# A fifth slot in the third weight ring, routing tiles in the loop's buffers, and a residual added at another place, in a hybrid mixer and mixture-of-experts layer

## The chip, the core and the metric

The kernel runs on one core of a Trainium2 chip. The metric is the device time of one execution in microseconds (us), the median of several runs; a profile of one execution says where that time goes. PE is TensorE, PEld its weight load, DVE is VectorE, ACT is ScalarE, POOL is GpSimd, and SP is the engine whose queue (SPq) issues nearly all loads here.

## What is computed

One decoder layer for 256 tokens of width 1024, in float32. The first sub-layer mixes tokens (a gated linear attention and a pooling branch) and ends with a LayerNorm; the second is a mixture of 64 small experts with a shared expert, and ends with another LayerNorm. Cut to what matters here:

```python
h = layer_norm(ALPHA * x + mixer(x), ln1_g, ln1_b)          # first sub-layer
scores = sigmoid(h @ w_router)                              # (256, 64)
biased = scores + router_bias
# the best 4 of 8 groups of experts, by the sum of a group's two best,
# then the best 8 experts in them; weights = scores of these, normed, * 2.5
routed = sum over experts e of
         gate[t, e] * (silu(h @ w_exp_gate[e]) * (h @ w_exp_up[e])) @ w_exp_down[e]
shared = (silu(h @ w_sh_gate) * (h @ w_sh_up)) @ w_sh_down
out = layer_norm(ALPHA * h + routed + shared, ln2_g, ln2_b)
```

Each expert has three matrices of 1024 x 256 or 256 x 1024, 1 MB each, so the experts alone are 192 MB that have to be read once.

## The kernel before

All weights come in pieces of 1 MB in one fixed list (`loads`), the order in which they are used: the columns of w_in, the matrices of the branches, w_sh_gate, and then for the experts two at a time `gate`, `gate`, `up`, `up`, and the `down` matrices four at a time. The class Ring hands each next load to the slot that has come free: `open` fills a pool of slots, `done` says that a load is used up and issues the next one of the list into its slot. The slots are those of ring1 (8, one of them held by x at first), ring2 (6, opened when the branches' tiles are gone), ring3 (NR3 = 4, L814, opened when the first sub-layer's last buffers are gone) and xt (2, tiles xTh and xTl), 20 in all; one more load, `lent`, borrows another buffer once. All these issues stand in SP's queue, in the order of the program, and each waits until what its slot held before has been read. ring3 is closed at q = 4 (L1202): its slots aren't filled again, and from q = 7 their memory holds `overflow()` (a branch for the case that an expert has more than 32 tokens of a tile, L1078, not taken with these inputs) and the tiles of the shared expert (`shp`).

Between the sub-layers stands the routing: router scores, the bias, group choice and the choice of 8 experts run on DVE as a chain of small steps (L855 to L881), their tiles lie in a pool of their own, `mid`, and PE meanwhile computes the shared expert's gate. Then the first `gather` (L895) picks the tokens of eight experts by matrix products.

The loop (L1183) has 16 rounds q of four experts. Each round has two `gate_up` (64 matmuls each, L1031), the transposes of their result (`hidden_t`), the `down` products of the round before in two halves of the columns (L1056), whose results ACT and DVE split into two parts (L1061, L1062), and `scatter` (L1073, L1074), which adds them to four PSUM banks `acc[t, half]`, one for each tile t of 128 tokens and each half of the columns. What is to be scattered waits in the list `ready`, and `flush` empties it. In rounds 2 to 5 `residual(t, c)` (L975) also puts ALPHA * h into `ready`, for 256 columns at a time; it needs ln1_g and ln1_b with the same row on all 128 partitions, and `load_rows(c)` (L990) fetches them so from HBM, two loads for each c, at q = 0 (c = 0 and 1), 3 and 4. The other rows, of ln2, are loaded to one partition (`lnr`, L1226, at q = 12) and spread by POOL (L1231).

The last round's downs are done in three pieces of columns, 512, 256 and 256. Both tiles are taken in turn, piece by piece (L1248). `scatter` takes a half's statistics as soon as it is whole (L1076); then come mean and deviation, and four halves are normalised on three engines (L1268) and stored from SP's queue.

Of the kernel before, what the change touches and what calls it, by code (L numbers as in the profile page):

```python
# [16 lines left out]
NQ = E // 4  # L17
# [5 lines left out]
NR1, NR2, NR3 = 8, 6, 4  # L23
# [3 lines left out]
ROWS, RES = {0: (0, 1), 3: (2,), 4: (3,)}, {2: 0, 3: 1, 4: 2, 5: 3}  # L27

C_ID, C_MASK, C_TRI, C_IOTA, C_RC, C_SLOT, C_OWN = 0, 128, 320, 448, 480, 544, 545
C_COLS = 549  # L30
# [80 lines left out]
def body(ctx, tc, A, out, dbg=lambda *a: None, stop=None):  # L111
# [96 lines left out]
    cst = keep.tile([128, C_COLS], FT, name="cst")  # L208
# [19 lines left out]
    onesb = keep.tile([128, 128], BF, name="onesb")  # L228
# [6 lines left out]
    gla = tc.alloc_tile_pool(name="gla", bufs=1)  # L235

# [15 lines left out]
    for n in range(2):  # L252
# [3 lines left out]
    nc.sync.dma_start(cst[:, C_MASK:], A["cst"][:, C_MASK:])  # L256
# [6 lines left out]
    nc.sync.dma_start(wr, A["w_router"][0].rearrange("(p k) e -> p k e", k=8))  # L263
    nc.sync.dma_start(rbias, bass.AP(tensor=A["router_bias"].tensor, offset=A["router_bias"].offset,
                                     ap=[[0, 128], [1, E]]))
    V.memset(one_c, 1.0)
    V.memset(eps_rms, RMS_EPS)
    V.memset(eps_ln, LN_EPS)
    V.memset(onesb, 1.0)
    G.tensor_copy(identb, ident)  # L270
    G.tensor_copy(trib, cst[:, C_TRI:C_TRI + 128])
# [78 lines left out]
    def gla_steps():  # L350
# [25 lines left out]
        def small_scores(lv, lhs, rhs):  # L376
            p = bank("b", (8, 32), "gs")
            for jt in range(2):
                for h in range(H):
                    for b in range(4):  # L380
                        t0 = 128 * jt + 32 * b
                        PE.matmul(p[32 * b:32 * b + 32, 4 * jt + h], lhs[:, h, t0:t0 + 32],
                                  rhs[:, h, t0:t0 + 32], start=True, stop=True,
                                  tile_position=(0, 32 * b))
            m = cst[:, None, C_MASK + 32 * lv:C_MASK + 32 * (lv + 1)].to_broadcast([128, 8, 32])
# [145 lines left out]
    def pool_steps():  # L531
        yield "late2"
        sw, pl, pm, mx = {-1: uT}, {}, {}, {}
        for i in range(8):
# [10 lines left out]
            if 0 <= i - 1 < 4:  # L545
# [3 lines left out]
                V.tensor_mul(pl[n][:, :16], t[:, n, :16], cst[:, C_RC + 16 * n:C_RC + 16 * (n + 1)])  # L549
# [269 lines left out]
    sc = mid.tile([128, 2, E], FT, name="sc")  # L819
# [23 lines left out]
    pr = mid.tile([128, 2, 8, 4, 8], FT, name="pr", tag="pr", bufs=1)  # L843
    gs = mid.tile([128, 2, 8], FT, name="gs")
    top = mid.tile([128, 2, 8], FT, name="top")
    gr = mid.tile([128, 2, 8], FT, name="gr")
    pen = mid.tile([128, 2, 8], FT, name="pen")
    mx8 = mid.tile([128, 2, 8], FT, name="mx8")
    mbr = moe.tile([128, 2, 16, 8], FT, name="mbr", tag="PT", bufs=2)
    mb, mr = mbr[:, 0], mbr[:, 1]  # L850
    sel = mid.tile([128, 2, E], FT, name="sel")
    selb = mid.tile([128, 2, E], BF, name="selb")
# [79 lines left out]
    PE.matmul(pc[:1], onesb[:, 0:1], selb, start=True, stop=True)  # L932
# [18 lines left out]
    ssum = mid.tile([128, 2], FT, name="ssum")  # L951
    gt = mid.tile([128, 2, E], FT, name="gt")
# [21 lines left out]

    def residual(t, c):  # L975
# [4 lines left out]
        tmp = moe.tile([128, FF], FT, name="tmp", tag="sg", bufs=1).rearrange("p (q k) -> p k q", k=8)  # L980
# [202 lines left out]
    for q in range(NQ):  # L1183
        last = q == NQ - 1
        for c in ROWS.get(q, ()):
            load_rows(c)
        if q in RES:
            ready.append(residual(0, RES[q]))
# [8 lines left out]
        if q in RES:  # L1197
            ready.append(residual(1, RES[q]))
        if q == 7:
            rest.release()  # L1200
        if q == CLOSE3 - 3:
            ring.closed.add("w3")  # L1202
        if q == CLOSE3:
# [16 lines left out]
        if q == SH_DOWN:  # L1220
            shared_down()
            shp.release()
# [34 lines left out]
    flush()  # L1257
    for t in range(2):
        m = mv[:, t]
        V.bn_aggr(m[:, 0:2], st2[:, t])  # L1260
        S.activation(m[:, 2:3], m[:, 1:2], AF.Sqrt, bias=eps_ln)
    for t in range(2):
        m = mv[:, t]
        V.reciprocal(m[:, 3:4], m[:, 2:3])
        if t:
            V.scalar_tensor_tensor(m[:, 4:5], m[:, 0:1], -1.0, m[:, 3:4], op0=OP.mult, op1=OP.mult)

    def finish(t, n, engines):  # L1268
        m, ot, hs_ = mv[:, t], o[t][:, halves[n]], halves[n]
        if engines is None:  # L1270
            V.scalar_tensor_tensor(ot, acc[t, n], m[:, 0:1], g2[:, hs_], op0=OP.subtract, op1=OP.mult)
            V.scalar_tensor_tensor(ot, ot, m[:, 3:4], b2[:, hs_], op0=OP.mult, op1=OP.add)
        else:
            S.activation(ot, acc[t, n], AF.Identity, scale=m[:, 3:4], bias=m[:, 4:5])
            engines[0].tensor_mul(ot, ot, g2[:, hs_])
            engines[1].tensor_add(ot, ot, b2[:, hs_])

    finish(1, 0, (G, G))
    finish(0, 0, None)
    finish(0, 1, None)  # L1280
    finish(1, 1, (V, V))
    for t in range(2):
        for hs_ in halves:
            nc.sync.dma_start(out[0, 128 * t:128 * (t + 1), hs_], o[t][:, hs_])
# [26 lines left out]
```

## Time and profile before

| | us |
|---|---|
| median of 3 runs (lowest, highest) | 701.03 (700.68, 701.27) |
| the profiled execution | 701.09 |
| its span, first to last instruction | 699.2 |
| PE busy in the span | 675.0 (97%) |
| DVE, ACT, POOL busy | 291.4, 228.0, 60.9 |
| DMA: bytes, mean rate | 243.07 MB, 348 GB/s |

A busy PE isn't a PE that decides: matmuls overlap, and their ends are modelled. The page of the profile has the span in 40 slices, a chain of work that is followed back from the last instruction to what released each step, and groups of instructions; other views give single instructions in order of time, or the busy time of each engine in chosen windows with the granted TensorE clock (PEclk, 1.00 is full), the mean busy share of the 16 DMA engines, and the rate.

### The profile page before, as it was taken

How to read it: one execution, taken by the hardware profiler on the slowest of the kernel's cores; microseconds unless marked ns; L12 is line 12 of the kernel's file. 1: busy time of each engine (PE TensorE's matmuls, PEld its weight loads, DVE VectorE, ACT ScalarE, POOL GpSimd, SP SyncE). 2: the span in 40 equal slices, each digit the busy share in tenths (PEclk: the TensorE clock that was granted, in tenths of full speed). 3: DMA queues.
4: the chain of work that ended last, by engine and by line, in shares of the span. 5: the costliest groups of instructions: out<-in, count | busy, mean ns of one | idle time of the engine just before them, and what ended most of it. 6: DMA issues, size and time to landing. Idle time of an engine off the chain costs nothing.

```text
span 699.2 us, 13708 instructions
## 1 busy us (share of the span) xinstructions
PE 675.0 (97%) x5948; PEld 478.3 (68%) x5948; DVE 291.4 (42%) x476; ACT 228.0 (33%) x352; POOL 60.9 (9%) x51
## 2 busy tenths in 40 slices
PE   8999999999999999999999999999999899899993
PEld 8999999999999756556556546555645555364541
DVE  3688745946676523354343123311212221121216
ACT  4554646764444213123223113210312221131232
POOL 1053404600002000000000002000000000000001
PEclk9999999999999999999999999999999999999998
DMA  9995543499677799999999999999999999999981
GB/s 284 295 350 155 175 127 122 128 382 420 238 267 299 274 425 412 422 419 406 420 418 421 418 419 419 419 423 418 419 421 419 420 419 419 422 419 416 403 294 60
DMA packets 67889, 243.07 MB, mean 348 GB/s; under 512 B 6994, under 2 KB 37458, under 8 KB 44020
## 3 DMA queue, kind: packets, MB, share of 16 engines
q1 hardware_dynamic: 67684, 242.11, 88.3%
q8 instruction: 47, 0.77, 0.5%
q10 hardware_dynamic: 144, 0.07, 0.1%
q14 instruction: 14, 0.11, 0.0%
HBM read 241.11 MB, written 1.05 MB: 346 GB/s over the span
## 4 chain that ended last, share of the span: by engine, by line
PE 59%; DMA 38%; DVE 2%; issue 0%; ACT 0%; SPq 0%; DVEq 0%
PE pgu L1031 15%; DMA w<-in_w_exp_up 15%; DMA w<-in_w_exp_down 12%; DMA w<-in_w_exp_gate 9%; PE py L1056 7%; PE proj L291 6%; PE proj L293 6%; PE proj L292 6%; DMA xTl<-in_w_exp_down 3%; PE pgat L905 2%; PE acc L1073 1%; PE yg L293 1%; PE yg L292 1%; PE yg L291 1%; PE mix L291 1%; PE mix L292 1%
## 5 line engine op out<-in xcount | busy, mean ns | idle before, releaser
L1031 PE MATMUL pgu<-w,xg 128*64 128x256 f32 x1824 | 228.8, 381 | 6.8 <-DMA w<-in_w_exp_up 6.0
L1031 PEld LDWEIGHTS pgu<-w,xg 128*64 128x64 f32 x1824 | 142.5, 137 | 94.2 <-ACT Y L1061 11.7
L1056 PE MATMUL py<-w,ht 128*32 128x512 f32 (+1 forms) x904 | 121.7, 591 | 2.3 <-DMA w<-in_w_exp_down 1.8
L288 DVE TENSOR_TENSOR sl<-w,sh 128x1024 fp32r<-128x1024 f32 (+1 forms) x63 | 80.3, 1282 | 41.9 <-ACT sh L287 41.7
L1038 DVE TENSOR_TENSOR h<-sg,pgu 128x256 f32<-128x256 f32 x32 | 13.5, 422 | 187.7 <-ACT sg L1037 128.5
L1062 DVE SCALAR_TENSOR_TENSOR Y<-py,gsl,Y 128x512 fp32r<-128x512 f32 (+1 forms) x66 | 48.1, 734 | 96.2 <-ACT Y L1061 96.1
L291 PE MATMUL proj<-xTh,sh 128*128 128x256 f32 x288 | 83.0, 288 | 0.3 <-ACT sh L287 0.3
L293 PE MATMUL proj<-xTh,sl 128*128 128x256 f32 x288 | 81.5, 283 | 0.2 <-DVE sl L288 0.2
L1061 ACT ACTIVATE Y<-py,gsl 128x512 fp32r<-128x512 f32 (+1 forms) x66 | 44.2, 673 | 114.4 <-PE py L1056 114.3
L292 PE MATMUL proj<-xTl,sh 128*128 128x256 f32 x288 | 81.0, 281 | 0.0
L1037 ACT ACTIVATE sg<-pgu 128x256 f32<-128x256 f32 x32 | 12.3, 384 | 198.1 <-PE pgu L1031 198.1
L287 ACT ACTIVATE sh<-w 128x1024 fp32r<-128x1024 f32 (+1 forms) x63 | 64.3, 1028 | 35.0 <-PE proj L293 13.4
L1056 PEld LDWEIGHTS py<-w,ht 128*32 128x32 f32 x904 | 31.6, 111 | 57.1 <-issue 48.8
L291 PEld LDWEIGHTS proj<-xTh,sh 128*128 128x128 f32 x288 | 54.1, 188 | 1.1 <-ACT sh L287 0.5
L292 PEld LDWEIGHTS proj<-xTl,sh 128*128 128x128 f32 x288 | 54.6, 190 | 0.3 <-DVE xTl L288 0.2
L293 PEld LDWEIGHTS proj<-xTh,sl 128*128 128x128 f32 x288 | 53.9, 187 | 0.4 <-DVE sl L288 0.4
L1056 PE MATMUL py<-xTl,ht 128*32 128x512 f32 (+1 forms) x104 | 44.1, 562 | 0.0
L1031 PE MATMUL pgu<-xTh,xg 128*64 128x256 f32 x144 | 32.7, 380 | 0.0
L777 DVE TENSOR_SCALAR xg<-pgat,cols_sb 128x512 f32<-128x512 f32 x32 | 25.7, 809 | 13.9 <-PE pgat L905 11.5
L905 PE MATMUL pgat<-P,xl 128*128 128x256 f32 x128 | 30.6, 283 | 0.3 <-DVE xl L941 0.3
L905 PE MATMUL pgat<-P,xh 128*128 128x256 f32 x128 | 30.3, 283 | 0.0
L779 ACT ACTIVATE xg<-pgat,cols_sb 128x512 f32<-128x512 f32 x32 | 24.7, 777 | 17.3 <-PE pgat L905 17.3
(269 smaller groups left out, 948.5 us busy)
## 6 DMA issues: line engine op xcount, KB each, us to landing
w<-in_w_exp_gate SPq DMA_DIRECT2D x59, 1024.0 KB, 15.8
w<-in_w_exp_up SPq DMA_DIRECT2D x55, 1024.0 KB, 19.0
w<-in_w_exp_down SPq DMA_DIRECT2D x49, 1024.0 KB, 19.8
w<-in_w_in SPq DMA_DIRECT2D x21, 1024.0 KB, 7.2
xTh<-in_w_exp_up SPq DMA_DIRECT2D x6, 1024.0 KB, 17.3
xTl<-in_w_exp_down SPq DMA_DIRECT2D x5, 1024.0 KB, 16.2
w<-in_w_exp_down SPq DMA_DIRECT2D x9, 512.0 KB, 15.4
w<-in_w_gla_up SPq DMA_DIRECT2D x4, 1024.0 KB, 10.9
```

The costliest lines, as they stand in the source:

```text
L287: S.activation(hi, src, AF.Copy)
L288: eng.tensor_sub(lo, src, hi.bitcast(FT))
L291: PE.matmul(o, ah, bh, start=start, stop=False, skip_group_check=shared_bank)
L292: PE.matmul(o, ah, bl, start=False, stop=False, skip_group_check=shared_bank)
L293: PE.matmul(o, al, bh, start=False, stop=stop, skip_group_check=shared_bank)
L777: V.tensor_scalar(dst, p, g1T[:, k:k + 1], b1T[:, k:k + 1], op0=OP.mult, op1=OP.add)
L779: S.activation(dst, p, AF.Identity, bias=b1T[:, k:k + 1], scale=g1T[:, k:k + 1])
L905: PE.matmul(p[k][:, t].rearrange("p e s -> p (e s)"), part[:, t, k], P8[o][:, t].rearrange("p e s -> p (e s)"), start=part is xh, stop=par ...
L1031: PE.matmul(p[64 * c:64 * c + 64, g], xg[:, k, e].rearrange("p t s -> p (t s)"), w[c][:, k], start=k == 0, stop=k == 7, tile_position=(0, ...
L1056: PE.matmul(p[32 * c:32 * c + 32], HT[2 * q + c // 2][:, j, c % 2, t], ring.get(li["down", 4 * q + c])[:, j, cs], start=j == 0, stop=j == ...
L1061: S.activation(hi, p, AF.Copy, scale=g)
L1062: V.scalar_tensor_tensor(lo, p, g, hi.bitcast(FT), op0=OP.mult, op1=OP.subtract)
```

## The change

- `NR3` is 5: ring3 has a fifth slot. Room for it comes from smaller constants (the part that only the first sub-layer needs, `cst1`, moves to the branches' pool `right`), from `rbias`, which lies in R1's first half until R1 is written, and from `mid`, which is gone: the routing's tiles lie in buffers that the loop uses later (`ht`, `PT`, the rest of the tile of x2T).
- The router's bias is loaded ahead of the router's weights; the constants come in two loads instead of one; a one-column tile of ones is set besides the 128x128 one.
- `load_rows` and its eight loads are gone. At q = 7, behind `overflow()`, two loads bring ln1_g and ln1_b to one partition, and POOL spreads them to all (`spread`).
- `residual` runs at q = 9 and 10, on 512 columns at a time, and takes h from the shared expert's tiles `SH[t]`, so that the addition of xh and xl falls away; `shp` is released at q = 11 instead of 10.
- At the end tile 0's three pieces come before tile 1's second and third, tile 0's mean and deviation are taken while tile 1's last piece is computed, and the four halves are spread over the engines in another way.

```diff
-NR1, NR2, NR3 = 8, 6, 4
+NR1, NR2, NR3 = 8, 6, 5
-ROWS, RES = {0: (0, 1), 3: (2,), 4: (3,)}, {2: 0, 3: 1, 4: 2, 5: 3}
+RES = 9
...
-    rbias = keep.tile([128, E], FT, name="rbias")
     R1 = keep.tile([128, 2, E], FT, name="R1")
+    rbias = R1[:, 0]
...
-    nc.sync.dma_start(cst[:, C_MASK:], A["cst"][:, C_MASK:])
+    nc.sync.dma_start(cst1, A["cst"][:, C_KEPT:])
+    nc.sync.dma_start(cst[:, C_IOTA:], A["cst"][:, C_IOTA:C_KEPT])
...
-    mid = tc.alloc_tile_pool(name="mid", bufs=1, reuse_waits="tile")
+    ht = [moe.tile([128, n], dt, name="mid", tag="ht", bufs=3) for n, dt in ((256, FT), (512, BF), (256, FT))]
+    mbr = moe.tile([128, 2, 16, 8], FT, name="mbr", tag="PT", bufs=2)
+    scgt = moe.tile([128, 2, 2, E], FT, name="scgt", tag="PT", bufs=2)
...
     def residual(t, c):
-        qs = slice(32 * c, 32 * (c + 1))
-        lo, hi = (rest.tile([128, 256], FR, name=n) for n in ("reslo", "reshi"))
+        qs = slice(64 * c, 64 * (c + 1))
+        tmp = shp.tile([128, 8, 64], FT, name="tmp")
+        hi, lo = (shp.tile([128, 512], FR, name=n) for n in ("reshi", "reslo"))
-        V.tensor_add(tmp, xh[:, t, :, qs].bitcast(FT), xl[:, t, :, qs].bitcast(FT))
-        for n, op in (("g", OP.mult), ("b", OP.add)):
-            V.tensor_tensor(tmp, tmp, rows1[n, c].rearrange("p (q k) -> p k q", k=8), op)
+        g, b = (rows1[n].rearrange("p (q k) -> p k q", k=8)[:, :, qs] for n in "gb")
+        V.tensor_mul(tmp, SH[t][:, :, qs], g)
+        V.tensor_add(tmp, tmp, b)
         S.activation(hv, tmp, AF.Copy, scale=ALPHA)
         V.scalar_tensor_tensor(lv, tmp, ALPHA, hv.bitcast(FT), op0=OP.mult, op1=OP.subtract)
-        return None, t, slice(256 * c, 256 * (c + 1)), hi, lo
+        return None, t, halves[c], hi, lo
...
-        for c in ROWS.get(q, ()):
-            load_rows(c)
-        if q in RES:
-            ready.append(residual(0, RES[q]))
+        if RES <= q < RES + 2:
+            ready.append(residual(0, q - RES))
+        if q == RES + 2:
+            shp.release()
...
+            one = shp.tile([1, 2, D], FT, name="rowone")
+            for i, n in enumerate("gb"):
+                nc.sync.dma_start(one[:, i], A["ln1_" + n])
+                rows1[n] = shp.tile([128, D], FT, name="row" + n)
+            spread([rows1[n] for n in "gb"], one)
...
-    for cs in pieces_of(NQ - 1):
-        for t in range(2):
-            flush(1)
-            ready.append(down(NQ - 1, t, cs))
-    done_downs(NQ - 1)
...
-    finish(1, 0, (G, G))
-    finish(0, 0, None)
-    finish(0, 1, None)
-    finish(1, 1, (V, V))
+    c0, c1, c2 = pieces_of(NQ - 1)
+    for t, cs in ((0, c0), (1, c0), (0, c1), (0, c2), (1, c1)):
+        flush(1)
+        ready.append(down(NQ - 1, t, cs))
+    flush(1)
+    moments(0)
+    scales(0)
+    ready.append(down(NQ - 1, 1, c2))
+    done_downs(NQ - 1)
+    normed(0, 1)
+    affine2(0, 1, G)
+    centre(0, 0)
+    flush()
+    moments(1)
+    shift(0, 0)
+    scales(1)
+    normed(1, 1)
+    centre(1, 0)
+    shift(1, 0)
+    affine2(1, 1, V)
```

Here `moments` is the mean and the square root, `scales` the reciprocal and one small product, `centre` and `shift` are DVE's two steps on a half, `normed` is one ACT step, and `affine2` a multiplication and an addition on the engine named.

## Rows read from the trace of the kernel before

**Rows 1.** The page, the span in 40 equal slices: PE's busy tenths, and GB/s.
```profile
PE   8999999999999999999999999999999899899993
...
GB/s 284 295 350 155 175 127 122 128 382 420 238 267 299 274 425 412 422 419 406 420 418 421 418 419 419 419 423 418 419 421 419 420 419 419 422 419 416 403 294 60
```

**Rows 2.** The chain that ended last: start in us, length in us, what.
```profile
381.74 7.06 PE pgu L1031 x64
...
401.02 19.68 DMA w<-in_w_exp_up
...
665.63 3.67 PE pgu L1031 x30
```

**Rows 3.** Windows: busy us (instructions) of each engine, PEclk, DMA share, GB/s.
```profile
401.00:677.00 276.00, 265.63 (x2174) 152.30 (x2175) 62.33 (x117) 57.75 (x103) 7.22 (x4) 0.99 1.01 415
```

**Rows 4.** Windows as before, ahead of the loop, at its start and at the end.
```profile
227.00:231.00 4.00, 3.67 (x29) 3.38 (x29) 3.56 (x7) 0.21 (x1) 0.00 (x0) 1.00 0.56 162
...
235.00:242.00 7.00, 7.00 (x72) 4.52 (x70) 2.51 (x11) 1.36 (x3) 0.00 (x0) 1.00 0.70 207
277.00:278.00 1.00, 1.00 (x12) 0.68 (x10) 0.97 (x3) 0.00 (x0) 0.00 (x0) 1.00 0.91 344
...
681.50:682.00 0.50, 0.50 (x16) 0.26 (x8) 0.50 (x1) 0.00 (x0) 0.00 (x0) 1.00 0.00 0
```

**Rows 5.** SP's queue in order of time: start, us to the row's end, issues.
```profile
217.58 11.32 SPq L84 DMA_DIRECT2D w<-in_w_exp_up  x2
230.31 0.33 SPq L84 DMA_DIRECT2D w<-in_w_exp_gate  x1
234.91 0.34 SPq L995 DMA_DIRECT2D rowg<-in_ln_g  x1
...
236.90 0.38 SPq L84 DMA_DIRECT2D w<-in_w_exp_gate  x1
...
266.74 0.80 SPq L84 DMA_DIRECT2D w<-in_w_exp_up  x2
275.48 1.75 SPq L84 DMA_DIRECT2D w<-in_w_exp_down  x4
```

**Rows 6.** Windows as before, where the later row loads land.
```profile
315.00:320.00 5.00, 5.00 (x47) 3.24 (x44) 0.04 (x1) 0.32 (x1) 0.00 (x0) 1.00 1.01 378
345.00:355.00 10.00, 10.00 (x88) 5.08 (x86) 2.04 (x4) 2.14 (x4) 0.00 (x0) 1.00 1.01 414
```

**Rows 7.** The tile lnr: ns min/median/max, first and last start in us.
```profile
L1226 SPq DMA_DIRECT2D lnr<-in_ln_g x1: 293/293/293, 581.5 to 581.5; - x1
L1227 SPq DMA_DIRECT2D lnr<-in_ln_b x1: 232/232/232, 584.0 to 584.0; - x1
L1231 POOL PARTITION_BROADCAST g<-lnr x1: 1302/1302/1302, 592.8 to 592.8; - x1
```

**Rows 8.** The tile tmp of residual(), same columns and then the shapes.
```profile
L983 DVE TENSOR_TENSOR tmp<-tmp,rowg x8: 635/653/655, 277.6 to 363.7; 128x256 f32<-128x256 f32 x8
...
L984 ACT ACTIVATE reshi<-tmp x8: 672/677/699, 279.0 to 365.1; 128x256 fp32r<-128x256 f32 x8
```

**Rows 9.** The end in order of time: start, us, engine, line, out<-in [idle before <-releaser].
```profile
682.92 0.42 PE L1056 MATMUL py<-w,ht 128*32 128x256 f32 x3
...
686.93 0.47 ACT L1061 ACTIVATE Y<-py,gsl 128x256 fp32r<-128x256 f32 x1 [0.96 <-PE py L1056]
...
687.83 1.29 DVE L1076 BATCH_NORM_STATS2 st<-acc 128x6 f32<-128x512 f32 x2
...
692.87 1.59 POOL L1276 TENSOR_TENSOR o<-o,b 128x512 f32<-128x512 f32 x1
693.26 1.74 DVE L1275 TENSOR_TENSOR o<-o,g 128x512 f32<-128x512 f32 x1
695.04 0.69 DVE L1276 TENSOR_TENSOR o<-o,b 128x512 f32<-128x512 f32 x1
```

**Rows 10.** Loads issued from 330 to 360 us: KB each, median us to landing.
```profile
w<-in_w_exp_gate SPq DMA_DIRECT2D x3, 1024.0 KB, 15.6
```

More of the change, by code (lines that the diff above doesn't have):

```diff
@@ L26 @@
 CLOSE3, SH_X2, SH_UP, SH_DOWN, TAIL = 7, 8, 9, 10, 12
[L27 to L30 removed]
+RES = 9
+C_ID, C_IOTA, C_SLOT, C_OWN, C_MASK, C_TRI, C_RC = 0, 128, 160, 161, 165, 357, 485
+C_KEPT, C_COLS = 165, 549
 def constants():
@@ L206, in bank @@
         return v
-    cst = keep.tile([128, C_COLS], FT, name="cst")
+    cst = keep.tile([128, C_KEPT], FT, name="cst")
     ident = cst[:, C_ID:C_ID + 128]
@@ L227, in body @@
     trib = keep.tile([128, 128], BF, name="trib")
-    onesb = keep.tile([128, 128], BF, name="onesb")
+    ones1 = keep.tile([128, 1], BF, name="ones1")
     ring1 = ctx.enter_context(tc.tile_pool(name="ring1", bufs=NR1))
@@ L235, in body, with cst_of @@
     gla = tc.alloc_tile_pool(name="gla", bufs=1)
+    onesb = right.tile([128, 128], BF, name="onesb")
+    cst1 = right.tile([128, C_COLS - C_KEPT], FT, name="cst1")
+    def cst_of(c, n):
+        return cst1[:, c - C_KEPT:c - C_KEPT + n]
     x = ring1.tile([128, 2048], FT, name="x", tag="w1", bufs=NR1).rearrange("p (t d) -> p t d", t=2)
@@ L269, in body @@
     V.memset(onesb, 1.0)
+    V.memset(ones1, 1.0)
     G.tensor_copy(identb, ident)
-    G.tensor_copy(trib, cst[:, C_TRI:C_TRI + 128])
+    G.tensor_copy(trib, cst_of(C_TRI, 128))
     def split(src, n, tag="s", pool=splits, bufs=3):
@@ L842, in body @@
     bi = moe.tile([128, 2, 8, 2, 8], FT, name="bi", tag="h", bufs=1)
[L843 to L849, printed above, removed]
+    pr = early[:, 2048:2560].rearrange("p (t g r e) -> p t g r e", t=2, g=8, r=4)
+    gs, top, gr, pen = (ht[0][:, n:n + 16].rearrange("p (t g) -> p t g", g=8) for n in range(192, 256, 16))
+    mx8 = ht[2][:, 0:16].rearrange("p (t g) -> p t g", g=8)
+    ssum = ht[2][:, 16:18]
     mb, mr = mbr[:, 0], mbr[:, 1]
-    sel = mid.tile([128, 2, E], FT, name="sel")
-    selb = mid.tile([128, 2, E], BF, name="selb")
+    sel = ht[0][:, 0:128].rearrange("p (t e) -> p t e", e=E)
+    selb = ht[1][:, 0:128].rearrange("p (t e) -> p t e", e=E)
     P8 = {}
@@ L931, in body @@
     pc = bank("a", (2, E), "pcount")
-    PE.matmul(pc[:1], onesb[:, 0:1], selb, start=True, stop=True)
+    PE.matmul(pc[:1], ones1, selb, start=True, stop=True)
     shared_in("w_sh_gate", psh, x2T, tiles[1], (1,), range(SPLIT2, 8))
@@ L948, in body @@
     dbg("R1", R1)
-    ssum = mid.tile([128, 2], FT, name="ssum")
-    gt = mid.tile([128, 2, E], FT, name="gt")
     V.tensor_copy(sel, selb)
@@ L1196, in body @@
             build_p(q // 2 + 1, 1)
[L1197 to L1200, printed above, removed]
+        if RES <= q < RES + 2:
+            ready.append(residual(1, q - RES))
         if q == CLOSE3 - 3:
@@ L1230, in body @@
         if q == TAIL + 1:
-            G.partition_broadcast(g2, lnr[:, 0])
-            G.partition_broadcast(b2, lnr[:, 1])
+            spread([g2, b2], lnr)
         build_pt(q)
@@ L1247, in body, with moments @@
     st2 = tail.tile([128, 2, 2, 6], FT, name="st2")
-    for cs in pieces_of(NQ - 1):
-        for t in range(2):
-            flush(1)
-            ready.append(down(NQ - 1, t, cs))
-    done_downs(NQ - 1)
     mv = tail.tile([128, 2, 6], FT, name="mv2")
     o = [tail.tile([128, D], FT, name=f"o{t}") for t in range(2)]
[L1257 to L1262, printed above, removed]
+    def moments(t):
+        V.bn_aggr(mv[:, t, 0:2], st2[:, t])
+        S.activation(mv[:, t, 2:3], mv[:, t, 1:2], AF.Sqrt, bias=eps_ln)
@@ L1263, in body, with scales @@
+    def scales(t):
         m = mv[:, t]
         V.reciprocal(m[:, 3:4], m[:, 2:3])
[L1265 to L1276, printed above, removed]
@@ L1278, in body, with centre, shift @@
-    finish(1, 0, (G, G))
-    finish(0, 0, None)
-    finish(0, 1, None)
-    finish(1, 1, (V, V))
+        V.scalar_tensor_tensor(m[:, 4:5], m[:, 0:1], -1.0, m[:, 3:4], op0=OP.mult, op1=OP.mult)
+    def centre(t, n):
+        V.scalar_tensor_tensor(o[t][:, halves[n]], acc[t, n], mv[:, t, 0:1], g2[:, halves[n]],
+                               op0=OP.subtract, op1=OP.mult)
+    def shift(t, n):
+        V.scalar_tensor_tensor(o[t][:, halves[n]], o[t][:, halves[n]], mv[:, t, 3:4], b2[:, halves[n]],
+                               op0=OP.mult, op1=OP.add)
@@ new lines, in normed, with affine2, store @@
+    def normed(t, n):
+        S.activation(o[t][:, halves[n]], acc[t, n], AF.Identity, scale=mv[:, t, 3:4], bias=mv[:, t, 4:5])
+    def affine2(t, n, eng):
+        eng.tensor_mul(o[t][:, halves[n]], o[t][:, halves[n]], g2[:, halves[n]])
+        eng.tensor_add(o[t][:, halves[n]], o[t][:, halves[n]], b2[:, halves[n]])
+    def store(t, n):
+        nc.sync.dma_start(out[0, 128 * t:128 * (t + 1), halves[n]], o[t][:, halves[n]])
+    c0, c1, c2 = pieces_of(NQ - 1)
+    for t, cs in ((0, c0), (1, c0), (0, c1), (0, c2), (1, c1)):
+        flush(1)
+        ready.append(down(NQ - 1, t, cs))
@@ L1282, in body @@
+    flush(1)
[14 more added lines that the diff above has]
+    affine2(1, 1, V)
     for t in range(2):
-        for hs_ in halves:
-            nc.sync.dma_start(out[0, 128 * t:128 * (t + 1), hs_], o[t][:, hs_])
+        for n in range(2):
+            store(t, n)
     for pool in (tail, moe, ring2, xt):
```

23 lines of the change are left out of this document (8 added, 15 removed).

## The prediction

> **What bounds the kernel now.** I read the 40 slices first, then the chain that ended last, then windows along it. In the slices [rows 1] the reader is to see three stretches of the GB/s line, each slice 17.5 us: a first part that falls to 122 to 175 GB/s and stays uneven to about 240 us, then a plateau of mostly 418 to 422 that holds to about 660 us, then a short end. The chain [rows 2] says when the plateau matters: up to 401 us it runs over PE, each gate_up taking 7.06 us, and from 401.02 to 665.63 us it is made of nothing but expert loads. So PE eats a store of loaded weights until 401 us, and after that the date of every load decides. TensorE isn't the bound there: from 401 to 677 us it is busy 265.6 of 276 us, so 10.4 us of idle time are left in it [rows 3]; the granted clock is 0.99 of full speed there, so the clock plays no part. A megabyte (1024 KB) on the plateau costs 1.049 MB / 0.42 MB per us = 2.5 us. What the change saves in transfer time, or in DMA idle time ahead of the plateau, comes out of the end, until the 10.4 us are used up; what it saves on PE ahead of 401 us does not.
>
> **Part 1, the fifth slot of ring3.** Before the loop starts the transfers run dry. SP issues the four loads of ring3 from 216.3 us on, the last at 217.58; the second load of that row starts only when w_sh_gate's slot is free (the row ends at 228.9), then x's slot follows at 230.31 [rows 5]. From 227 to 231 us the engines moved 162 GB/s x 4 us = 0.65 MB where the plateau would have moved 1.68 [rows 4]: 1.03 MB were missed, which is just one more slot. Its memory lies past the branch tiles that ring3's other slots wait for, so I take the fifth load to be issued right behind the fourth. The loads come in one fixed order and SP issues them in it, so every later load moves up by one slot. Is the lead kept? At 277 us the transfers almost run dry again (344 GB/s, share 0.91 [rows 4]), because SP had no free slot between the pair of 266.74 and 275.48 us [rows 5]: with 8 + 6 + 4 + 2 = 20 slots they were as far ahead of PE as they can be, and with 21 they can be one megabyte further. So this part gives 2.5 us, and with it everything ahead of 277 us: a second saving there finds no slot. Bounds: 0 (the lead is given back later) to 2.5.
>
> **Part 2, the LayerNorm rows of the first sub-layer.** Eight loads go away, each of 128 rows of 1 KB, 131 KB, the same KB for every partition; two loads of 4 KB to one partition come instead. The first four stand at 234.9 to 236.5 us [rows 5], ahead of the limit at 277 us, so I cost their removal at nothing; that they do cost time is shown by 235 to 242 us, where with a share of 0.70 only 207 GB/s were moved [rows 4], and this is a rival below. The last four, from q = 3 and 4, lie on the plateau. From 315 to 320 us the rate is 378 GB/s [rows 6]: 1.89 MB less two row loads of 0.131 leaves 1.63 MB of weights where 2.10 would have come, 0.47 MB or 1.1 us. From 345 to 355 us it is 414 [rows 6]: 4.14 less 0.26 is 3.88 against 4.20, 0.32 MB or 0.8 us. Together 1.9 us. By their bytes alone, 0.52 MB, it would be 1.2 us, and by the dearer pair twice 2.2; I take 1.9, since it is the sum of what both stretches show.
> The Trainium skill speaks against the difference: "DMA: Bandwidth & Descriptors", Specifications, puts the least transfer for full rate at 512 bytes, so rows of 1 KB should cost their bytes alone, and the sum would be 0.7 us smaller, 696.8. The stretch at 378 GB/s [rows 6] disagrees with that, and I go by the stretch.
> The two new loads come in SP's queue at q = 7, behind the branch of overflow() and ahead of the loads that gate_up(15) frees; those wait for them. The nearest rows are the two 4 KB loads of lnr: each took one turn of SP, 2.5 us [rows 7], while the slices around 582 us stay at 419 GB/s and above [rows 1]. At q = 4 a load took 15.6 us to land, some six megabytes deep [rows 10], so two turns (5 us) are covered; without the cover they would cost up to 5 us, and I take 0. The two broadcasts on POOL, 1.30 us each [rows 7], stand in an otherwise empty queue some 20 us ahead of their use.
>
> **Part 3, residual() at q = 9 and 10.** Eight pieces of 256 columns become four of 512, each without the first addition. A DVE step of 128x256 takes 0.65 us and the ACT step 0.68 [rows 8]; twice as wide, with the same strides, I take 1.3 and 1.36, so the chain of one piece is 2 x 1.3 + 1.36 + 1.3 = 5.3 us. Its cover is the gate_up of 7.06 us [rows 2] that stands ahead of the scatter that needs it. Queued behind it on DVE are the PT tile and the evictions of the next downs, on ACT the Silu of gate_up, which is later anyway. PE's work is the same, sixteen matmuls of 256 columns becoming eight of 512; it leaves the stretch where PE decides and comes to one with idle time, and as a row of 256 columns takes 0.42 us at most [rows 9], it is under 6.7 us out of 10.4, which PE has gained ahead of 401. Cost 0.
>
> **Part 4, routing in the loop's buffers, bias and constants.** No instruction is added to the routing chain. The first write of the loop into each such buffer comes behind a whole gate_up after the last routing step, 7.06 us [rows 2]; were that cover gone, the loop would start later by a DVE step (under 1 us), and the 10.4 us of PE would take that as well. The bias is loaded one place sooner; the constants come in two loads instead of one, and there is one more memset of a column. PE is busy 90% or more from the second slice on [rows 1], while the rate falls from the fourth, so the head is PE's and I cost them at 0; without that cover one more issue on SP would be about 0.4 us, the length of such an issue [rows 5].
>
> **Part 5, the end.** On PE only the order of the last four downs changes: tile 0's third piece goes ahead of tile 1's second. On the clock of before it is needed at 682.92 us [rows 9]; the last bytes were in before 681.5 [rows 4], and both move together. Then, on the clock of before: tile 0's last statistics run once DVE has evicted tile 1's second piece, about 686.5 to 687.2 (0.65 each [rows 9]); its mean and scale are ready at 688.05. Their Sqrt stands on ACT ahead of the eviction of tile 1's third piece, which slips from 686.93 to 687.66; DVE evicts to 688.65, centres tile 0 (0.75) to 689.4, takes tile 1's statistics to 690.1, mean 690.3, Sqrt 690.6. Shift of tile 0 waits for POOL's multiplication (from 688.95 on, as long as its addition of 1.59) at most 0.4 us and ends at 691.4, scales 691.75, centre 692.5, shift 693.25, two steps of 0.69 to 694.6. Before, the last step ended at 695.73 [rows 9]: 1.1 us less. Against it: a multiplication on DVE beside POOL's addition took 1.74 us, and the addition after it 0.69 [rows 9]: it ended 0.54 us after POOL's step. If a small step of scales(1), which reads two SBUF operands, has to wait likewise for POOL's addition (1.59 us, here 691.4 to 693.0), the end comes at 696.0, 0.3 us later than before. Between -0.3 and 1.1 I take 0.6, since the small step isn't in the rows beside a POOL step.
> The Trainium skill ("SBUF — State Buffer", SBUF: two separate sides) has the pair of ports that VectorE and GpSimd share as an exclusive lock for a whole instruction; by that rule the end gains nothing. The multiplication of 1.74 us agrees with it.
>
> **Sum.** 2.5 + 1.9 + 0 + 0 + 0.6 = 5.0 us. The profiled execution took 701.09 us (span 699.2), the median is 701.03; 701.1 - 5.0 = 696.1 us. The transfers' 4.4 us fit in the 10.4 of PE.
>
> **Rivals.**
> More: the lead isn't held at 277 us. Without the first rows the two loads of 236.9 us start some 0.4 us sooner and reach full rate about 2.4 us after their issue, as the load of 228.6 did [rows 4, 5]; by 242 us 1.65 MB of weights instead of 1.45 - 0.52 = 0.93 would be in, 1.7 us. With the end at its best: 693.9. Against it stands the dry second at 277.
> Given back: ring3 closes at q = 4, and five slots instead of four aren't filled again. If the 16 others then hold the transfers, the megabyte of lead is lost and 2.5 us are left: 698.6. For it: PE still decides there. Against it: the 15.6 us to landing [rows 10].
> The lock at the end: 701.1 - 4.1 = 697.0.
> The change doesn't do it: the fifth load is held in SP's order or the rate falls elsewhere, and only the end gains: 700.5.
> Slower: the 512-wide strided steps cost twice as much per element. Then a residual's chain is 10.6 us, 3.5 more than its cover, four times 14 us on PE in q = 9 and 10; 6.0 of them go into the idle time that is left, 8.0 come out at the end: 701.1 - 5.0 + 8.0 = 704.1. It decides once the chain is longer than 7.06 + (6.0 + 5.0) / 4 = 9.8 us. Against it: the steps of before lie between 0.64 and 0.66 us, whatever the piece [rows 8].
>
> **How the numbers follow.** Forecast 0.52 (alone 694.7 to 697.5), more 0.15, given back 0.13, the lock 0.08, no effect 0.07, slower 0.05. The range reaches from just under the second to just above the third, 693.5 to 699.0, and leaves out the last two and the tails. This kernel's times lie within 0.1%, so about 0.2%, 1.4 us, can be told from no change: faster 0.88, same 0.07, slower 0.05.
>
> **What would show it.** In the changed profile: five loads issued at once after 216 us and no gap from 227 to 231; 277 us as dry as before or drier; no row loads, and 420 GB/s from 310 to 355 us; the chain entering the loads a few us after 401, since PE got faster ahead of it while the loads come 4.4 us sooner; idle time of PE down to about 6 us; at the end the last DVE step 9 us after the last eviction's Sqrt or less. I am wrong if PE's idle time is gone (then PE decides), if the DMA share falls under 0.98 after 340 us, or if PE waits for reshi or reslo at q = 9.

## The result and the profile after

The changed kernel takes 691.05 us (median of 4 runs, 690.21 to 691.55), the kernel before beside it 701.15 (700.68 to 701.78): a ratio of 0.985, 95% interval 0.984 to 0.987, or 10.1 us less. The forecast was 696.1, 5.0 us less, and its range ended at 693.5. The profiled execution of after took 691.21 us, its span is 689.4.

The slices of after, GB/s, each slice 17.2 us:

```profile
GB/s 283 308 349 163 180 123 124 142 385 420 249 265 299 348 421 381 422 420 419 418 419 421 420 419 419 411 420 421 418 420 422 418 421 417 421 419 417 408 328 64
```

Set beside [rows 1], the slice at 224 to 241 us is fuller (348 for 274), a dip to 381 has come at 259 to 276 us, the 406 at 315 to 332 us is gone, and a 411 stands where the two new row loads land.

The chain that ended last, its part where it enters the loads and where it leaves them:

```profile
538.33 7.06 PE pgu L1033 x64
545.39 0.12 PE pht L1047
545.51 19.84 DMA w<-in_w_exp_gate
...
641.63 15.29 DMA xTl<-in_w_exp_up
656.92 0.04 issue
656.97 3.67 PE pgu L1033 x30
```

Loads now decide from 545.51 us on, not from 401.02, but for a stretch from 600.22 to 621.03 us in which the chain runs over PE once more (left out above). The last load is in at 656.92, not 665.63 [rows 2]: 8.7 us sooner. From there to the end of the span it is 689.4 - 656.9 = 32.5 us, 33.6 before. So 8.7 us came ahead of the end and 1.1 in it, together the 9.8 us by which the two spans differ.

Windows of after (columns as in [rows 3]):

```profile
401.00:677.00 276.00, 267.71 (x2219) 151.97 (x2218) 78.56 (x133) 63.16 (x109) 9.65 (x6) 1.00 0.99 405
227.00:231.00 4.00, 3.84 (x32) 3.35 (x34) 3.35 (x7) 2.94 (x5) 0.00 (x0) 1.00 0.97 346
...
265.00:275.00 10.00, 10.00 (x90) 6.37 (x90) 4.74 (x6) 4.49 (x6) 0.00 (x0) 1.00 0.92 353
277.00:278.00 1.00, 1.00 (x13) 0.66 (x10) 0.00 (x0) 0.00 (x0) 0.00 (x0) 1.00 1.01 426
315.00:320.00 5.00, 5.00 (x40) 4.37 (x37) 2.04 (x3) 2.78 (x5) 0.00 (x0) 1.00 1.02 423
345.00:355.00 10.00, 10.00 (x93) 5.21 (x94) 1.50 (x2) 1.38 (x2) 0.00 (x0) 1.00 1.02 420
430.00:435.00 5.00, 5.00 (x50) 2.65 (x44) 1.50 (x2) 1.09 (x2) 2.48 (x2) 1.00 1.01 397
```

PE is left with 8.3 us of idle time where it had 10.4 [rows 3]; about 6 was forecast. Its busy time in the whole span is 6.5 us shorter as well (675.0 us before, 668.5 now). Added up by tile, each matmul up to the next one's start, 3.2 us of this are the projections, of which more below, and 3.3 the gate_ups and downs, whose instructions are the same; likely that is waiting for weights which the trace counts as busy, so the idle time alone says too little of what the loads gained.

The gap at 227 us is nearly filled (346 for 162 GB/s [rows 4]), and the late row loads are gone (423 and 420 for 378 and 414 [rows 6]). The us at 277 isn't dry any more (426 for 344 GB/s [rows 4]), against the forecast; the stretch in which the slots limit the loads has moved ahead of it, to 265 to 275 us (353 GB/s, share 0.92). Before had there:

```profile
265.00:275.00 10.00, 10.00 (x86) 6.67 (x82) 4.12 (x6) 4.57 (x7) 0.00 (x0) 1.00 1.01 416
```

SP's queue in after, from the loads of ring3 on:

```profile
213.11 0.33 SPq L84 DMA_DIRECT2D w<-in_w_exp_down  x1
213.49 0.90 SPq L84 DMA_DIRECT2D w<-in_w_exp_gate  x2
214.43 1.14 SPq L84 DMA_DIRECT2D w<-in_w_exp_up  x2
...
264.01 9.60 SPq L84 DMA_DIRECT2D w<-in_w_exp_down  x4
```

The fifth load goes out right behind the fourth, as forecast: the pair at 214.43 takes 1.14 us where the pair of before took 11.32 [rows 5]. But the whole row begins 3 us sooner: it is at 214.43, and was at 217.58. Nothing in the prediction moves a load ahead of the loop by 3 us, and of the change only the loads of the bias and the constants stand there. The work ahead of that row is PE's, most of it projections (`proj`: products of x and the columns of w_in, both split into a high and a low part, xTh and xTl, sh and sl). Some projection matmuls out of PE's rows in order of time, of before and then of after, with the first and the last one:

```profile
7.93 0.38 PE L291 MATMUL proj<-xTh,sh 128*128 128x256 f32 x1 [0.31 <-ACT sh L287]
...
24.16 0.28 PE L291 MATMUL proj<-xTh,sh 128*128 128x256 f32 x1
24.52 0.29 PE L291 MATMUL proj<-xTh,sh 128*128 128x256 f32 x1
24.88 0.28 PE L291 MATMUL proj<-xTh,sh 128*128 128x256 f32 x1
...
158.63 0.28 PE L293 MATMUL proj<-xTh,sl 128*128 128x256 f32 x1
```
```profile
8.00 0.39 PE L300 MATMUL proj<-xTh,sh 128*128 128x256 f32 x1 [0.31 <-ACT sh L296]
...
24.23 0.28 PE L300 MATMUL proj<-xTh,sh 128*128 128x256 f32 x1
24.57 0.28 PE L300 MATMUL proj<-xTh,sh 128*128 128x256 f32 x1
24.91 0.28 PE L300 MATMUL proj<-xTh,sh 128*128 128x256 f32 x1
...
100.43 0.28 PE L300 MATMUL proj<-xTh,sh 128*128 128x256 f32 x1
100.78 0.28 PE L300 MATMUL proj<-xTh,sh 128*128 128x256 f32 x1
101.14 0.28 PE L300 MATMUL proj<-xTh,sh 128*128 128x256 f32 x1
...
155.49 0.28 PE L302 MATMUL proj<-xTh,sl 128*128 128x256 f32 x1
```

Two more matmuls (of xTl and sl) stand between every two of the rows at 24 us and at 100 us, so before it is 0.36 / 3 = 0.120 us from one start to the next, and after 0.34 / 3 = 0.113, later (at 100 us) 0.71 / 6 = 0.118. From the first start to the last it is 150.7 us before and 147.5 after: 3.2 us, all that ring3's row has gained. Instructions, shapes and order are the same, and PEclk is 1.00 in both. There are 1056 such matmuls, so it is 3 ns each. What differs is where the tiles lie: the smaller constant tiles let everything that is allocated behind them on the left side of SBUF slide down by 2016 bytes, sh and sl (the split weights) among it, while xTh and xTl on the right side stay.

### The profile page after: what moved, and what is told of

The parts are those of the page before. It is cut to its first block, busy times and chain, and to the rows that moved or that the text cites. A ratio compares the mean times of both kernels' runs of the same rounds, so it can differ in the third digit from the quotient of the medians.

```text
span 689.4 us, 13660 instructions
## 1 busy us (share of the span) xinstructions
PE 668.5 (97%) x5940; PEld 471.8 (68%) x5940; DVE 287.8 (42%) x458; ACT 227.8 (33%) x348; POOL 66.8 (10%) x53
## 5 line engine op out<-in xcount | busy, mean ns | idle before, releaser
L1033 PE MATMUL pgu<-w,xg 128*64 128x256 f32 x1840 | 222.4, 381 | 1.3 <-DMA w<-in_w_exp_gate 1.3
L1033 PEld LDWEIGHTS pgu<-w,xg 128*64 128x64 f32 x1840 | 138.7, 137 | 86.1 <-ACT Y L1063 11.7
L1058 PE MATMUL py<-w,ht 128*32 128x512 f32 (+1 forms) x912 | 120.2, 580 | 1.8 <-DMA w<-in_w_exp_down 1.4
L1058 PE MATMUL py<-xTh,ht 128*32 128x512 f32 x80 | 36.3, 594 | 0.0
L1033 PE MATMUL pgu<-xTl,xg 128*64 128x256 f32 x128 | 29.2, 381 | 3.8 <-DMA xTl<-in_w_exp_up 3.8
```

The lines of the kernel that those rows point to most:

```text
L1033: PE.matmul(p[64 * c:64 * c + 64, g], xg[:, k, e].rearrange("p t s -> p (t s)"), w[c][:, k], start=k == 0, stop=k == 7, tile_position=(0, ...
L1058: PE.matmul(p[32 * c:32 * c + 32], HT[2 * q + c // 2][:, j, c % 2, t], ring.get(li["down", 4 * q + c])[:, j, cs], start=j == 0, stop=j == ...
```

## The experiments

Every run has the kernel before beside it on the same chip (medians 700.69 to 700.78 us). The runs of one kernel spread over 1 us or so, hence a few tenths between two medians say nothing. A label that begins with a_ or s4_ is an edit of after (s4_ with four slots), one with b_ an edit of before.

**Each part alone.** Four slots instead of five in the kernel after:

```diff
-NR1, NR2, NR3 = 8, 6, 5
+NR1, NR2, NR3 = 8, 6, 4
```

> The kernel after with four slots in ring3 instead of five; all else as after, 691.05 us. Theory 1, as in the prediction: the fifth slot is one megabyte of lead, 2.5 us, so 693.5. Theory 2: the slot is where the 5 us came from that the prediction lacked, so 697 to 698.5. Theory 3: the lead is given back when ring3 closes, so 691.1.

Measured: 693.58 us (693.13 to 694.61), so the slot is worth 2.5 us (theory 1), with a few tenths of doubt, as after stood in another comparison. A second pair with five slots and four, a_left0 and s4_eq128 further down, both with the slow projections (but the right side placed differently), gives 696.31 - 694.26 = 2.1. The dry stretch is back, here with the 4 us of it on this kernel's clock, and below it the same window of after:

```profile
223.00:227.00 4.00, 3.70 (x29) 3.11 (x28) 3.52 (x7) 0.00 (x0) 0.00 (x0) 1.00 0.58 174
```
```profile
223.00:227.00 4.00, 3.82 (x31) 3.23 (x29) 3.62 (x10) 0.00 (x0) 0.00 (x0) 1.00 1.02 420
```

It is 246 GB/s x 4 us = 0.98 MB that the slot brings in, the 1.03 MB of the prediction.

The end of after in the kernel before:

> The kernel before with the end of after alone (order of the last downs, moments, the four halves over the engines). Theory 1, from the two traces: from the last late load's gate_up to the end it was 33.5 us before and 32.5 after, so 1.0 us less, 700.1. The prediction's own term, 0.6, gives 700.5. The lock between DVE and POOL: 701.1 to 701.4.

Measured: 699.73 us against 700.69, ratio 0.9987 (0.9978 to 0.9996): 1.0 us. Its rows at the end:

```profile
690.07 1.59 POOL L1274 TENSOR_TENSOR o<-o,b 128x512 f32<-128x512 f32 x1
...
690.65 1.03 DVE L1259 SCALAR_TENSOR_TENSOR mv<-mv 128x1 f32<-128x1 f32 x1
...
693.76 0.69 DVE L1274 TENSOR_TENSOR o<-o,b 128x512 f32<-128x512 f32 x1
```

The small step of `scales(1)` on one column takes 1.03 us and ends, at 691.68, as POOL's addition does (691.66); the same step for tile 0, with POOL idle, takes 0.16. So the wait of the prediction's lower bound is there, 0.9 us long. Even so the last step ends at 694.45, before at 695.73 [rows 9].

The row loads of the first sub-layer's LayerNorm, the four of q = 0 and the four of q = 3 and 4, each pair of pairs left out alone:

```diff
+            if c in (0, 1):        # the other run: (2, 3)
+                G.memset(rows1[n, c], 1.0)
+                continue
             src = A["ln1_" + n]
```

> The kernel before without the four row loads of q = 0: the tiles rowg and rowb for c = 0 and 1 are set to ones by POOL instead of being loaded, so half the columns of the residual are computed with ones in place of ln1_g and ln1_b. Theory 1, the prediction's step: these loads lie ahead of the second at 277 us in which the transfers were as far ahead as the slots let them be, so 0 us. Theory 2, the prediction's rival: with them gone 1.7 us more of weights are in by 242 us, and that lead is kept, so 1.7 us less than before.

Measured: 699.90 us against 700.78, ratio 0.9986 (0.9978 to 0.9995): 0.9 us, between the theories. Windows of before and then of this run:

```profile
225.00:235.00 10.00, 9.66 (x81) 8.29 (x81) 8.79 (x26) 4.02 (x6) 0.00 (x0) 1.00 0.83 315
235.00:245.00 10.00, 10.00 (x100) 6.53 (x98) 2.51 (x11) 1.36 (x3) 0.00 (x0) 1.00 0.80 274
275.00:280.00 5.00, 5.00 (x52) 3.09 (x46) 3.15 (x6) 1.36 (x2) 0.00 (x0) 1.00 0.98 395
```
```profile
225.00:235.00 10.00, 9.66 (x82) 8.21 (x82) 8.80 (x26) 4.03 (x6) 0.11 (x1) 1.00 0.81 286
235.00:245.00 10.00, 10.00 (x100) 6.54 (x98) 2.44 (x11) 1.26 (x3) 1.02 (x4) 1.00 0.85 328
275.00:280.00 5.00, 5.00 (x48) 3.19 (x46) 3.01 (x6) 1.36 (x2) 0.00 (x0) 1.00 0.81 303
```

By 245 us 6.14 MB came, all of it weights, where before 5.89 less 0.52 of rows came: 0.77 MB, 1.8 us at 0.42 MB per us. At 275 to 280 us (395 - 303) x 5 = 0.46 MB of that, 1.1 us, is given back, since the slots are full. 0.7 us remain.

> The kernel before without the four row loads of q = 3 and 4: rowg and rowb for c = 2 and 3 are set to ones by POOL instead, so the other half of the columns of the residual is computed with ones. Theory 1, the prediction's step, from the rates of 378 and 414 GB/s where they land: 1.9 us less than before. Theory 2, that they cost their bytes: 4 x 0.131 MB at 0.42 MB per us, 1.2 us less. Theory 3, that both pairs cost as the dearer: 2.2 us less or more. The four runs so far leave 3 to 3.6 us for all row loads and the rest together.

Measured: 698.27 us against 700.78, ratio 0.9963 (0.995 to 0.9975): 2.5 us, with 1.75 to 3.5 in the interval, so that 1.9 and 2.2 hold and the 1.2 us of the bytes alone don't. The stretches of [rows 6] are level:

```profile
315.00:320.00 5.00, 5.00 (x47) 3.32 (x42) 0.12 (x1) 0.58 (x2) 0.00 (x0) 1.00 1.01 419
345.00:355.00 10.00, 10.00 (x87) 5.10 (x84) 2.32 (x4) 2.14 (x4) 0.00 (x0) 1.00 1.01 419
```

The two new loads at q = 7, left out of after (the tile set to ones by POOL):

> The kernel after without its two row loads of q = 7: the one-partition tile is set to ones by POOL instead, so the residual is computed with ones in place of ln1_g and ln1_b. The prediction's step: their two turns of SP lie behind loads that are deep in the queue, so 0, 691.1. Theory 2, from the trace of after, 397 GB/s in the 5 us in which they land and 415 in the next against 420: 0.14 MB, 0.3 us, so 690.8. Theory 3: two whole turns of SP, 5 us, so 686.

Measured: 690.97 us, and 691.12 for after in the same comparison: no difference that could be told; in the trace 415 GB/s for 397 at 430 to 435 us, 0.09 MB or 0.2 us.

**The place of the operands.** In bytes behind a multiple of 128, sh and sl lie at 0 in the kernel before and at 32 in after; xTh and xTl at 96 in both. First the kernel before, with nothing but an unused tile added, on the left and on the right:

```diff
+    pad = keep.tile([128, 8], FT, name="pad")     # behind onesb: left side 32 bytes up
+    pad = xt.tile([128, 8], FT, name="pad")       # behind xTl, in the other run: right side 32 down
```

> The kernel before with 32 unused bytes behind its constant tiles, so that everything on the left side of SBUF, the split weights sh and sl among it, lies 32 bytes higher; no instruction changes. In the trace of before sh lies at a multiple of 64 bytes and xTh 32 behind one, and a projection matmul follows the last in 0.120 us; in after both lie 32 behind a multiple, and it is 0.113 to 0.118. Theory 1: the place of the operands sets that period, so the projections take 0.113 to 0.118 us here, the first load of ring3 is issued some 3.1 us sooner than at 216.26, and the time is 701.1 - 3.1 = 698.0. Theory 2: the earlier head of after comes from the order of its first loads or from the chip, so the period stays 0.120 and the time 701.1.

> The kernel before with 32 unused bytes behind xTl on the right side, so that xTh, xTl and ring2 lie 32 bytes lower, at a multiple of 64 as sh and sl do; no instruction changes. Theory 1a: what counts is that the two operands of a matmul have the same place within 64 bytes, so the period is 0.113 to 0.118 us and the time 698.0. Theory 1b: what counts is that sh and sl lie 32 bytes behind a multiple of 64, whatever xTh does, so 0.120 us and 701.1. Theory 2, neither: 701.1.

Measured: 697.73 us (697.3 to 698.21), 3.0 less than before; and 696.76 (696.48 to 697.88), 3.9 less. ring3's first load is issued at 213.41 and 212.56 us, as in after (213.11), not at 216.26. The projections of b_left32:

```profile
23.81 0.28 PE L292 MATMUL proj<-xTh,sh 128*128 128x256 f32 x1
24.15 0.28 PE L292 MATMUL proj<-xTh,sh 128*128 128x256 f32 x1
24.49 0.28 PE L292 MATMUL proj<-xTh,sh 128*128 128x256 f32 x1
```

0.113 us, without one instruction changed; from the first start to the last it is 147.2 us in b_left32 and 147.6 in b_right32, for 150.7 before. Theory 2 is out, and 1b too, as sh lies at 0 in the second run. Then the other way round, after with its left side 32 bytes lower (sh at 0 again), and with both sides lower:

```diff
-    small = keep.tile([128, 4], FT, name="small")
+    small = keep.tile([128, 5], FT, name="small")
-    ones1 = keep.tile([128, 1], BF, name="ones1")
+    ones1 = small[:, 4:5].bitcast(BF)[:, 0:1]
+    pad = xt.tile([128, 8], FT, name="pad")       # in the second run alone
```

> The kernel after with the one-column tile of ones put into a tile that is there already, so that everything on the left side of SBUF lies 32 bytes lower: sh and sl at a multiple of 64 bytes as in the kernel before, xTh and xTl 32 behind one as before. All other changes are kept. Theory 1: the place of the operands is worth 3.0 us here too (the kernel before gained 3.0 by it), so 691.1 + 3.0 = 694.1, a projection matmul each 0.120 us. Theory 2: the place is worth less with a fifth slot, since slots and not the head limit the loads: 691.1 to 692.5.

> The kernel after with both sides 32 bytes lower, left as in the run before and right by 32 unused bytes behind xTl: all four of sh, sl, xTh, xTl at a multiple of 64. Theory 1: only that both have the same place within 64 bytes counts, so 691.1 as after. Theory 2: both at a multiple of 64 is better than both 32 behind, as the kernel before came to 696.8 by the one and 697.7 by the other: 690.1.

Measured: 694.26 us (693.7 to 695.45), so the place is worth 3.2 us in after, the projections take 150.8 us again from first start to last, and ring3's first load goes out at 217.09; and 690.31 for both sides. That was repeated beside after:

> The kernel after once more, unchanged, so that the next run has it on the same chip: 691.1 us by every theory.

> The kernel after with sh, sl, xTh and xTl all at a multiple of 64 bytes, once more, beside the kernel after. It came to 690.3 where after had come to 691.05 in an earlier comparison. Theory 1: the difference is real, 0.7 us, as in the kernel before (696.8 against 697.7): 690.3. Theory 2: chance, so 691.1.

Measured: 691.12 and 690.65 us. Twice the version with both sides lower was the faster one, by 0.7 and 0.5, and the runs overlap (690.69 to 691.95 and 690.37 to 691.33), so it can't be called better than after.

Which distance between the two operands is fast? Two more with four slots, where there is room (right side 96 bytes lower and left 32; or left 32 higher), beside a_slots4 at 693.58:

> The kernel after with four slots in ring3, left side 32 bytes lower and right side 96 bytes lower, so that sh, sl, xTh and xTl all lie at a multiple of 128 bytes. With four slots and the places of after (32 and 96 bytes behind a multiple of 128) it was 693.6. Theory 1: the place within 64 bytes is all that counts, so a projection matmul each 0.113 to 0.118 us and 693.0 to 693.6. Theory 2: it is the place within 128 bytes, with a difference of 64 good and others not, so 0.120 us and 696.7. Theory 3: the same place within 128 bytes is better still, below 0.113 us, and under 692.

> The kernel after with four slots in ring3 and 32 bytes more of constants, so that sh and sl lie 64 and xTh and xTl 96 bytes behind a multiple of 128: 32 bytes apart in 128, where 64 has been fast (693.6 with four slots) and 0 (696.3) and 96 (by the kernel before) slow. Theory 1: only 64 is fast, so 0.120 us and 696.3. Theory 2: 32 is fast too, 0.113 to 0.118 us and 693.6.

Measured: 696.31 and 693.97 us. With all that was seen of the projections (us per matmul as the mean distance of their starts, in two stretches of time, and us from the first start to the last):

| kernel | sh, xTh behind a multiple of 128 | distance in 128 | 24 to 66 us | 68 to 156 us | first to last |
|---|---|---|---|---|---|
| before, a_left0 | 0, 96 | 96 | 0.118 to 0.119 | 0.120 | 150.7, 150.8 |
| s4_eq128 | 0, 0 | 0 | 0.120 | 0.120 | 151.1 |
| s4_diff32 | 64, 96 | 32 | 0.118 | 0.117 | 148.4 |
| b_left32, after, a_slots4 | 32, 96 | 64 | 0.114 | 0.118, 0.118, 0.117 | 147.2, 147.5, 147.1 |
| b_right32, a_both0 | 0, 64 | 64 | 0.114 | 0.118 | 147.6, 148.2 |

At distance 64 the same matmuls have two rates: 0.113 us in most groups up to 65 us and 0.118 in all later ones in after, with no operand moved and a granted clock of 1.00 throughout. In a_slots4 the step comes at 77 us. No run says why.

s4_eq128 has the same place within 64 bytes and is slow, so theory 1 of that run is out; 32 is fast, so "only 64" is out. If the distance were all, other matmuls would follow it: yg and yp stand at distance 0 in after, and so do the gathers (P8 over xh and xl). A tile of 64 bytes ahead of ogh, and the two gsl tiles ahead of PT, take them to 64:

```diff
+        pad2 = late2.tile([128, 16], FT, name="pad2")         # a_far_head
+    for _ in range(2):                                        # a_far_loop
+        moe.tile([128, 2], FT, name="gsl", bufs=2)
```

> The kernel after with 64 unused bytes ahead of ogh, so that ogh, ogl, mxh, mxl, mgh and mgl lie 64 bytes further behind a multiple of 128 than sh and sl; nothing else moves. In the trace of after the 288 matmuls yg and yp follow each other in 0.120 us, with both operands 32 bytes behind a multiple of 128. Theory 1: a distance of 64 in 128 between the two operands gives the faster period wherever 256 columns go over 128x128 weights, so 0.113 to 0.118 us here, 288 x 0.0065 at most 1.9 us, with some 0.3 us from mix, and the time 691.1 - 1.9 = 689.2 (689 to 690.4). Theory 2: the period of the projections hangs on something else that moved with them, so 0.120 us and 691.1.

> The kernel after with the two small gsl tiles ahead of PT, so that PT, h, P8 and sg lie 64 bytes higher, P8 64 further behind a multiple of 128 than xh and xl. A gather's 32 matmuls take 3.82 us in the trace of after, 0.119 each. Theory 1: 0.113 us, 3.6 us a gather, 0.2 us for each of the eight; TensorE no longer decides at the end, so only those ahead of 545 us come through in part: 690.1 to 691.1. Theory 2: 3.82 us as before and 691.1.

> Both of the two edits before together. Theory 1: 688.2 to 689.5, faster than after and than every kernel so far. Theory 2: 691.1.

Measured: 690.95, 691.37 and 690.64 us; none can be told from after. The groups of yg in after and in a_far_head (mean ns of one), and a gather in the chains of after and of a_far_loop:

```profile
L300 PE MATMUL yg<-ogh,sh 128*128 128x256 f32 x64 | 18.1, 283 | 0.0
```
```profile
L300 PE MATMUL yg<-ogh,sh 128*128 128x256 f32 x64 | 17.9, 280 | 0.0
```
```profile
423.97 3.82 PE pgat L914 x32
```
```profile
424.13 3.77 PE pgat L916 x32
```

They get faster: from one start to the next, yg and yp go from 0.120 to 0.118 us and the gather from 0.119 to 0.118. That is the slower of the two rates which the shifted projections have; the 1.9 us expected of a_far_head took the faster one. At 0.118 the 288 matmuls of yg and yp give 0.6 us, and the same edit slows `mix`, whose operands it moves too (512 columns, 0.229 to 0.233 us from one start to the next, 96 of them, 0.4 us), so no difference in time is left to see.

That a shift of one operand by 32 bytes changes the projections' time is shown, in both kernels and in both directions. The rule behind it isn't. What was seen of matmuls with 256 columns over 128x128 weights goes with the distance in 128 (0 and 96 slow, 32 and 64 faster), but that is four distances, `mix` goes the other way, and the step at 65 to 77 us stays open.

## Why the prediction was wrong, step by step

| part | gain forecast, us | gain measured, us | from |
|---|---|---|---|
| 1, fifth slot | 2.5 | 2.5 | a_slots4 |
| 2, late row loads | 1.9 | 2.5 | b_norows_late |
| 2, first row loads | 0 | 0.9 | b_norows_first |
| 2, two new loads | 0 | 0 to -0.2 | a_norowone |
| 5, the end | 0.6 | 1.0 | b_tail |
| 4, places of the tiles | 0, not seen | 3.2 | a_left0 |
| sum | 5.0 | 9.9 to 10.1 | 10.1 |

Parts 1, 4 and the two new loads were taken out of after, the others were put into before. Measured so they add up to the whole, and nothing is left for part 3 or the routing of part 4 that the runs could show. That the sum is met within 0.2 us is luck: the first row loads and the end are each known to some 0.6 us, the late row loads to 0.9.

**The step that failed** is part 4: it counted the instructions and loads that the smaller constants and the freed tiles add or move ("I cost them at 0"), and took it that an instruction that is not touched keeps its duration. 3.2 of the 5.1 missing us come from untouched matmuls whose operands were shifted. PE being busy 90% and more in the head was read rightly: just because that stretch is PE's, 3 ns on each of 1056 matmuls come out of it whole, and every later load, which waits for a slot that PE frees, moves with it. The prediction's opening, on what bounds the kernel, had ruled that out ("what it saves on PE ahead of 401 us does not" come out of the end); b_left32, which saves nothing else, ends 3.0 us sooner. The range had no room for it, as no rival changed the rate of TensorE. None of its signs of being wrong came either (the DMA share is 1.01 from 340 to 656 us, idle time is left, nothing waits for reshi): they looked at the loads and the residual, and the error was in the head. The other 1.9 us are sizes: 0.9 for the first row loads, 0.6 for the late ones, 0.4 at the end.

**Part 1** held with its mechanism and its size: the load goes out at once, the gap is filled, and the lead is kept when ring3 closes. The rival "given back" fell.

**Part 2** was right in the late loads; the stretch at 378 GB/s carried more than the bytes, as taken. It was wrong in the four early ones, taken at 0, which cost 0.9. The step "a second saving there finds no slot" is three fifths true: of 1.8 us, 1.1 are given back behind 275 us, but 344 GB/s and a share of 0.91 in one us [rows 4] showed that the slots were full there, not that a lead of any size had to be given back; some room was left. The rival "more" took 1.7 us for it, and half of that came.

**Part 3** held. The tiles of the residual in after:

```profile
L991 DVE TENSOR_TENSOR tmp<-xn,rowg x4: 1079/1084/1092, 459.6 to 503.4; 128x512 f32<-128x512 f32 x4
L992 DVE TENSOR_TENSOR tmp<-tmp,rowb x4: 1090/1090/1103, 460.8 to 504.5; 128x512 f32<-128x512 f32 x4
L993 ACT ACTIVATE reshi<-tmp x4: 1132/1136/1140, 461.9 to 505.7; 128x512 fp32r<-128x512 f32 x4
L994 DVE SCALAR_TENSOR_TENSOR reslo<-tmp,reshi x4: 1097/1099/1103, 463.1 to 506.9; 128x512 fp32r<-128x512 f32 x4
```

A piece is 1.08 + 1.09 + 1.14 + 1.10 = 4.4 us, less than the 5.3 taken, under its cover of 7.06, and no matmul waits for reshi or reslo. The rival "slower", at twice the cost per element, is out.

**Part 5** was right in the mechanism and too low by 0.4: the small step does wait for POOL's addition, as the lower bound had it, but POOL is done sooner than was worked out, since its multiplication takes 1.26 us (1.59 taken, from its addition):

```profile
680.45 1.26 POOL L1276 TENSOR_TENSOR o<-o,g 128x512 f32<-128x512 f32 x1 [91.40 <-issue]
...
681.79 1.59 POOL L1277 TENSOR_TENSOR o<-o,b 128x512 f32<-128x512 f32 x1
...
682.37 1.03 DVE L1262 SCALAR_TENSOR_TENSOR mv<-mv 128x1 f32<-128x1 f32 x1
```

The Trainium skill's lock ("SBUF — State Buffer", SBUF: two separate sides) agrees with this row as with the multiplication of before; the end gains 1.0 us in spite of it.

**The chain** was to enter the loads "a few us after 401" and does so at 545. The loads came 2.5 + 3.4 = 5.9 us nearer to PE; from 401 us on they fall behind PE by 10.4 us in 276 [rows 3], so by a rough estimate a lead of 5.9 us lasts 5.9 x 276 / 10.4 = 157 us longer, to 558. The sign was seen and the division wasn't made; no run tests the estimate.

## What to carry to other kernels

A change that resizes or moves a resident tile shifts all that is allocated behind it, so before it is priced, the addresses of the operands of the hottest matmuls are worth comparing, and in a stretch where TensorE decides a shift by 32 bytes is a cheap thing to try. When a sum falls short, look first whether rows of untouched work have the same length in both traces. Where PE frees the slots, a saving on PE ahead of the point where loads begin to decide moves the loads too and comes out of the end. A window that is dry by its share for one us says that slots limit the loads there, not how much room is left ahead of it; that is read from the whole stretch.

## What was not expected of the hardware

The projections (float32 operands split for the reduced type float32r, 256 columns over 128x128 weights) follow each other in 0.114 and later 0.118 us, or in 0.118 to 0.119 and later 0.120 us (24 to 66 and 68 to 156 us in after and before), at the same granted clock, by where moving and stationary operand lie in SBUF. Over all 1056 that is 3.1 to 4.0 us from the first start to the last, and the kernels differ by 2.7 to 3.9 us, in four pairs (700.7 and 697.7, 700.7 and 696.8, 694.3 and 691.1, 696.3 and 693.6). The Trainium skill ("SBUF — State Buffer", Who interferes with whom) gives TensorE two independent read ports, one for the moving operand and one for the weights. The place of the operands doesn't come into that; here it counts, and whether the two ports have to do with it no run shows. Inside the loop a gate_up whose weights are there takes 7.06 us in before, in after and in b_right32, so the effect wasn't seen in every shape.
